# A hybrid decoder block with 32 experts: expert weights in 2 MiB transfers with 16 KiB per partition, a reordered model dimension, and a rearranged end

## The chip, the cores and the metric

The kernel runs on one core of one Trainium2 chip. The metric is the device time of one execution in microseconds; the time before is the median of three runs. Inputs and outputs are float32, and all weights are read from HBM once per execution.

## The reference

256 tokens (with 16 learned meta tokens ahead of them) go through a mixer, a mixture of experts and a last norm:

```
h    = concat(meta, x)                                  # 272 x 1024
proj = rmsnorm(h, norm_mix) @ w_in                      # u, q, k, v, two gates
ssm  = gated(gelu(s5_ssm(u)) , w_glu)                   # state-space branch
attn = sliding_window_attention(q, k, v, sinks)         # 16 heads, window 128
h    = h + (sig(g1) * (ssm @ w_br_ssm) + sig(g2) * (attn @ w_br_attn)) @ w_out
t    = rmsnorm(h, norm_ffn)
top 4 of 32 experts per token by t @ w_router + b_router, softmax over the four
for each expert e, for its tokens:
    g, up = split(t @ w_gate_up[e] + b_gate_up[e])      # 1024 x 2048 weights
    hid   = min(g, 7) * sigmoid(1.702 * min(g, 7)) * (clip(up, -7, 7) + 1)
    y     = hid @ w_down[e] + b_down[e]                 # 1024 x 1024 weights
h    = h + sum over the four experts of gate * y
out  = rmsnorm(h, norm_final)[16:]
```

An expert's weights are 8 MiB (w_gate_up) and 4 MiB (w_down), 384 MiB for all 32.

## The kernel before, in words

The program is written in the order in which each engine runs it; nothing reorders it.

**Mixer.** Five groups of matrix products (`Early` and `Block`, 34 + 40 steps) take their weights as units of 1 MiB. In the loop of L1090 over the steps n, a `Block` of the last product (kind `out`, w_out) adds its result to the residual stream `xt` in one VectorE instruction for each 256 columns (`e2`, L868); ScalarE squares follow (`e3`), then transposes of `xt` (`turn_out`, L889) and the router's logits.

**Expert phase.** The loop of L1397 runs `gate_up` for expert e and, inside and behind it, `hid_T`, `down` and `combine` of the experts before. Only the first 64 slots of an expert are computed in this loop, which is enough here. `gate_up` (L1265) takes 8 units of weights, 128 rows of w_gate_up each; for each unit TensorE runs two products for the gate half and two for the up half, and these two lie side by side in the array's columns. `down` (L1296) takes 4 units of two chunks (128 rows of w_down each) into one PSUM bank `py`; ScalarE copies its lower half and VectorE its upper half to `y`. After each second expert `combine` (L1317) multiplies both experts' `y` by the gates (four products of 128 rows) and VectorE adds them to `acc`. `group` gathers the tokens of two experts (L1246) between the units.

**The ring (L79).** All weights, the mixer's too, are a list `todo` of 1 MiB units, and a list of free slots (8 KiB on each of 128 partitions). `pump` gives the first free slot to the next unit and issues its DMA on SyncE's queue. `done` puts a slot back when the program has issued the last product on its unit, so that the DMA into it waits on TensorE. A row of w_gate_up is 8 KiB, so a unit of it is one run of 8 KiB per partition (`gu_unit`, L187); a unit of w_down has two runs of 4 KiB per partition (`dn_unit`, L190). Slots are handed to the ring where the mixer's buffers come free (L247, L249, L262, L766, L1089, L1136 to L1151, L1156); 18 of them serve the experts, and two more (`aA` at 0 and `late_`) only until they become `acc` and `y`. The DMA completions use eight semaphores in turn, so at most eight of SyncE's transfers are under way: an issue waits for the landing of the eighth before it, and the queue is in order, so whatever stands behind a waiting issue waits too. The last expert's last 1 MiB comes as two transfers of 512 KiB (`dn_half`).

**End (L1420, L1444).** Behind the last `gate_up` come the end of `down(30)`, `hid_T(31)`, the products that spread norm_final over the partitions (`nf_banks`), `down(31)`, `combine` of experts 30 and 31, squares, a root on GpSimd, and for each of two token tiles two VectorE products, one ScalarE and one VectorE scaling and two output DMAs on SyncE (`last`, L1374).

The program as it stands before the change, where the diff touches it:

Of the kernel before, what the change touches and what calls it, by code (L numbers as in the profile page):

```python
# [73 lines left out]
class Slot:  # L74
    def __init__(self, ap):
        self.ap, self.keep = ap, True


class Ring:  # L79


    def __init__(self, eng):
        self.eng = eng
        self.todo, self.held, self.free, self.used = [], [], [], 0

    def add(self, parts):
        self.todo.append(parts)
# [50 lines left out]
def hybrid_block(ctx: ExitStack, tc: tile.TileContext, x, meta, norm_mix, w_in, lam_re, lam_im, log_dt,  # L138
# [48 lines left out]
    def gu_unit(e, k):  # L187
        return [(lambda t: t, w_gate_up[0, e, 128 * k:128 * k + 128, :])]

    def dn_unit(e, q):  # L190
        ap = w_down[0, e, 256 * q:256 * q + 256, :].rearrange("(c p) n -> p c n", p=128)
        return [(lambda t: t.rearrange("p (c n) -> p c n", c=2), ap)]

    def dn_half(e, c):
        return [(lambda t: t[:, :D], w_down[0, e, 128 * c:128 * c + 128, :])]

    for e in range(n_exp + 1):
        if e < n_exp:
            for k in range(8):
                ring.add(gu_unit(e, k))  # L200
        if e:
            for q in range(3 if e == n_exp else 4):
                ring.add(dn_unit(e - 1, q))
    for c in (6, 7):
        ring.add(dn_half(n_exp - 1, c))
# [41 lines left out]
    r0_slots = ring.slots([r0(0, U_)])  # L247
    nc.sync.dma_start(out=ct[:, 128:], in_=consts[:, 128:])
    r0_slots += ring.slots([r0(U_, U_)])  # L249
# [12 lines left out]
    r0_slots += ring.slots([r0(U_ * 2, U_)])  # L262
# [57 lines left out]
    T.transpose(aux[:, 0:32], rows[:32], ident[:32, :32])  # L320
    vecs = cp.tile([128, 32], F32, name="vecs")
    V.tensor_copy(vecs, aux[:, 0:32])
    nmix, dsk, nffn, bglu = (vecs[:, 8 * i:8 * i + 8] for i in range(4))
# [27 lines left out]
    wbuf = [pK.tile([128, 2, 8 * 128], F32R, tag="pb", name=n, bufs=2) for n in ("wh", "wl")]  # L351
# [133 lines left out]
    G.dma_start(out=wr, in_=w_router[0].rearrange("(k p) e -> p k e", p=128))  # L485
# [207 lines left out]
    gt.append(pB.tile([128, 8, NT], F32, name="gt0"))  # L693
    Z, Sc, X = (Arena(pB, U_, n) for n in ("Z", "Sc", "X"))
# [71 lines left out]
    r0_slots += ring.slots([r0(4 * U_, U_)])  # L766
# [28 lines left out]
    def act_pair(name):  # L795
# [3 lines left out]
        else:  # L799
            act[name] = [pK.tile([128, 8, NT], F32R, tag="pb", name=name + p, bufs=2) for p in "hl"]  # L800

    class Block:
# [5 lines left out]
        def hi(self):  # L808
# [46 lines left out]
        def e2(self):  # L855
# [124 lines left out]
    gt.append(pD.tile([128, 8, NT], F32, name="gt1"))  # L980
    Q, Y0 = Arena(pD, U_, "Q"), Arena(pD, U_, "Y0")
    W2 = Arena(pD, U_, "W2")
# [106 lines left out]
    ring.slots([Q(0, U_), Y0(0, U_)])  # L1089
    for n in range(B + 2):  # L1090
# [46 lines left out]
        if n == N + 1:  # L1137
            s_y = ring.slots([late_])[0]
            ring.slots([a(0, U_) for a in (Sc, W2)])
            r0_slots += ring.slots([r0(3 * U_, U_)])  # L1140
        if n == 17:
            ring.slots([Z(0, U_)])
# [381 lines left out]
```

## Time and profile before

| | us |
|---|---|
| median of three runs (1275.23 to 1277.87) | 1277.65 |
| the profiled execution | 1276.19 |
| its span, first to last instruction | 1274.4 |
| TensorE busy (share of the span) | 1188.9 (93%) |
| VectorE, ScalarE, GpSimd busy | 447.5, 224.7, 55.3 |
| HBM read | 443.31 MB, 350 GB/s over the span |

A busy TensorE is not TensorE at its peak: matmuls are pipelined and the ends in the profile are modelled. Each column of the page's timeline is a fortieth of the span, 31.9 us. The experts' weights are 403 of the 443 MB read. The granted clock was 0.994 over the span, which is the upper of TensorE's two levels (2.4 GHz) nearly throughout.

### The profile page before, as it was taken

What the parts mean: (1) busy time and instruction counts of PE and PEld (TensorE: products, weight loads), DVE (VectorE), ACT (ScalarE), POOL (GpSimd) and SP (SyncE); (2) the same over time, 40 slices, a digit from 0 to 9 for tenths busy, and PEclk for the clock granted to TensorE, in tenths of its full rate; (3) what the DMA queues carried; (4) which work ended last, traced back from release to release, by engine and by line L of the source; (5) the groups of instructions that cost most, each with busy time, mean ns of one, the idle gap of its engine ahead of it and who ended that gap; (6) DMA issues with size and microseconds to landing.
All of it is one profiled execution on the core that took longest, in us unless ns stands there. A gap on an engine that the chain in (4) does not pass through costs nothing.

```text
span 1274.4 us, 17188 instructions
## 1 busy us (share of the span) xinstructions
PE 1188.9 (93%) x7132; PEld 582.1 (46%) x7133; DVE 447.5 (35%) x995; ACT 224.7 (18%) x469; POOL 55.3 (4%) x86
## 2 busy tenths in 40 slices
PE   8989999999899999999989898989898989999985
PEld 6968778899333333333323232323232323333321
DVE  5978467675312231222213131212121222212212
ACT  3354366643000000000000000000000000000001
POOL 3019000000000000000000000000000000000000
PEclk9999989999999999999999999999999999999998
DMA  9925364898799999999999999999999999999994
GB/s 186 242 68 165 102 191 143 168 378 319 287 389 416 414 416 416 415 416 416 417 416 417 415 417 417 417 416 417 417 416 416 416 417 416 416 416 416 416 416 167
DMA packets 129285, 447.28 MB, mean 351 GB/s; under 512 B 26401, under 2 KB 62481, under 8 KB 96434
## 3 DMA queue, kind: packets, MB, share of 16 engines
q1 hardware_dynamic: 128768, 445.67, 90.5%
q8 instruction: 58, 0.95, 0.3%
q0 software_dynamic: 432, 0.45, 0.2%
q14 instruction: 25, 0.20, 0.0%
q10 hardware_dynamic: 2, 0.00, 0.0%
HBM read 443.31 MB, written 2.79 MB: 350 GB/s over the span
## 4 chain that ended last, share of the span: by engine, by line
DMA 51%; PE 41%; DVE 5%; ACT 2%; issue 1%; SPq 0%; POOL 0%; DVEq 0%; ACTq 0%
DMA r<-in_w_gate_up_dram 11%; DMA ws<-in_w_down_dram 6%; PE pgt L1273 6%; DMA Sc<-in_w_gate_up_dram 6%; PE py L1308 6%; PE pup L1273 6%; DMA X<-in_w_down_dram 5%; DMA Y<-in_w_gate_up_dram 5%; DMA Z<-in_w_gate_up_dram 5%; PE pu L419 4%; DMA Q<-in_w_down_dram 3%; DMA ws<-in_w_gate_up_dram 3%; PE pu L843 2%; PE pg L1246 2%; PE pu L844 2%; PE pu L845 2%
## 5 line engine op out<-in xcount | busy, mean ns | idle before, releaser
L1281 DVE TENSOR_SCALAR gs<-pgt 128x512 f32<-128x512 f32 x32 | 22.0, 687 | 235.2 <-PE pgt L1273 235.2
L1247 DVE TENSOR_TENSOR xw<-pg,vecs 128x256 f32<-128x256 f32 x64 | 27.1, 424 | 204.2 <-PE pg L1246 204.2
L1313 DVE COPY late__1936<-py 64x512 f32<-64x512 f32 x32 | 22.2, 695 | 189.2 <-ACT late__1936 L1312 189.2
L1246 PEld LDWEIGHTS pg<-aA,xt 128*128 128x128 f32 x512 | 61.9, 191 | 53.5 <-issue 49.4
L1273 PE MATMUL pgt<-r,xw 128*64 128x512 f32 x292 | 77.5, 609 | 6.6 <-DMA r<-in_w_gate_up_dram 5.9
L1246 PE MATMUL pg<-aA,xt 128*128 128x128 f32 x512 | 73.8, 287 | 2.6 <-DVE aA L1236 2.2
L1273 PE MATMUL pup<-r,xw 128*64 128x512 f32 x292 | 75.0, 592 | 0.0
L1308 PE MATMUL py<-r,hT 128*64 128x512 f32 x272 | 63.1, 595 | 5.1 <-DMA r<-in_w_down_dram 5.1
L1321 PE MATMUL pc<-late__1936,gT 128*128 128x512 f32 x128 | 62.2, 618 | 1.4 <-DVE late__1936 L1313 1.4
L1323 DVE TENSOR_TENSOR aA<-aA,pc 128x512 f32<-128x512 f32 x60 | 41.2, 687 | 56.5 <-PE pc L1321 56.5
L1312 ACT ACTIVATE late__1936<-py 64x512 f32<-64x512 f32 x32 | 18.9, 590 | 239.1 <-PE py L1308 239.1
L1293 ACT ACTIVATE hT<-pt 128x512 f32<-128x512 f32 x32 | 19.1, 597 | 208.8 <-PE pt L1291 208.8
L1263 ACT ACTIVATE gT<-pt 128x512 f32<-128x512 f32 x16 | 9.6, 597 | 255.8 <-PE pt L1262 255.8
L1282 ACT ACTIVATE sgm<-gs 128x512 f32<-128x512 f32 x32 | 20.0, 626 | 168.2 <-DVE gs L1281 168.2
L1273 PE MATMUL pgt<-ws,xw 128*64 128x512 f32 x168 | 44.6, 609 | 5.2 <-DMA ws<-in_w_gate_up_dram 4.8
L1308 PE MATMUL py<-ws,hT 128*64 128x512 f32 x168 | 40.0, 597 | 4.1 <-DMA ws<-in_w_down_dram 4.0
L1273 PE MATMUL pup<-ws,xw 128*64 128x512 f32 x168 | 43.2, 592 | 0.0
L1378 POOL TENSOR_TENSOR rsf<-ssf,nhalf 128x1 f32<-128x1 f32 x2 | 1.1, 554 | 946.8 <-DVE ssf L1377 946.8
L1308 PE MATMUL py<-gt,hT 128*64 128x512 f32 x160 | 38.1, 597 | 4.0 <-DMA gt<-in_w_down_dram 4.0
L1321 PEld LDWEIGHTS pc<-late__1936,gT 128*128 128x128 f32 x128 | 20.4, 188 | 43.1 <-DVE aA L1323 21.0
L1273 PEld LDWEIGHTS pup<-r,xw 128*64 128x64 f32 x292 | 20.9, 137 | 41.8 <-issue 41.8
L1308 PEld LDWEIGHTS py<-r,hT 128*64 128x64 f32 x272 | 19.0, 136 | 39.6 <-issue 25.1
(407 smaller groups left out, 2084.2 us busy)
## 6 DMA issues: line engine op xcount, KB each, us to landing
r<-in_w_gate_up_dram SPq DMA_DIRECT2D x73, 1024.0 KB, 19.7
ws<-in_w_gate_up_dram SPq DMA_DIRECT2D x42, 1024.0 KB, 20.0
r<-in_w_down_dram SPq DMA_DIRECT2D x34, 1024.0 KB, 20.0
gt<-in_w_gate_up_dram SPq DMA_DIRECT2D x22, 1024.0 KB, 20.0
Z<-in_w_gate_up_dram SPq DMA_DIRECT2D x21, 1024.0 KB, 20.1
Y<-in_w_gate_up_dram SPq DMA_DIRECT2D x21, 1024.0 KB, 20.1
W<-in_w_gate_up_dram SPq DMA_DIRECT2D x21, 1024.0 KB, 19.2
ws<-in_w_down_dram SPq DMA_DIRECT2D x21, 1024.0 KB, 20.1
```

The costliest lines, as they stand in the source:

```text
L419: T.matmul(pu, x_[:, k], y_[:, k, c:], start=(p + k == 0), stop=(p == len(pairs) - 1 and k == 7))
L843: T.matmul(pu, self.a[:, k], hi[:, k], start=(k == 0), stop=False)
L844: T.matmul(pu, self.a[:, k], lo[:, k], start=False, stop=False)
L845: T.matmul(pu, self.b[:, k], hi[:, k], start=False, stop=(k == 7))
L1246: T.matmul(pg[:, j], xt[:, t, 128 * (k + j):128 * (k + j) + 128], oh[:, t], start=(t == 0), stop=(t == 1))
L1247: V.tensor_tensor(xe[:, k:k + 2], pg, nffn[:, k:k + 2, None].to_broadcast([128, 2, n]), op=OP.mult)
L1273: T.matmul(p_[64 * hf:64 * hf + 64], lhs, rhs[:, c + 512 * hf:c + 512 * hf + 512], start=False, stop=(k == 7), tile_position=(0, 64 * hf), ...
L1281: V.tensor_scalar(g, pg, LIMIT, None, op0=OP.min)
L1308: T.matmul(py[64 * pp:64 * pp + 64], lhs, rhs[:, 512 * hf:512 * hf + 512], start=(c == -1), stop=(c == 7), tile_position=(0, 64 * pp), ski ...
L1313: V.tensor_copy(y[64:, 1 - odd], py[64:])
L1321: T.matmul(pc, gT[:, hf, t], y[:, hf], start=True, stop=True)
L1323: V.tensor_tensor(acc[:, t, cs_], (acc if started else xt)[:, t, cs_], pc, op=OP.add)
```

## The change

Four things. **(1)** An expert's weights come as 2 MiB transfers where two slots that lie side by side are free together: w_gate_up as four units of 256 rows, w_down as two units of 512 rows. In a unit partition p takes rows 2p and 2p + 1 of w_gate_up (or 4p to 4p + 3 of w_down), which is one run of 16 KiB. Slots are joined into seven pairs; four slots stay single, and a unit that meets no free pair is loaded as two halves into two single slots, with 8 KiB per partition. **(2)** Because a partition now holds neighbouring rows, the model dimension and the hidden dimension are read in another order. For the model dimension, the columns of w_out are taken with a stride where they are split (`Block.hi`, `lo`), `e2` becomes two VectorE instructions into PSUM and a ScalarE copy into `xt`, norm_ffn is loaded and transposed once more at the start (`nf4`), and w_router is loaded in the same order. For the hidden dimension, the clamps of `gate_up` read PSUM with a stride, and `down` writes `y` back in natural order by a strided copy. **(3)** Some slots reach the ring later (the pair of `Sc` and `Z` at n = 17, those of `W2`, `gt` and `X` at n = 33). **(4)** The end: `hid_T(31)` runs inside `down(30)`, the products on norm_final inside `gate_up(31)`; expert 30's share of the last combine runs inside `down(31)`, behind its chunks 1 and 3, as two products of 64 rows in the two row halves of the array; `down(31)` uses two PSUM banks; expert 31's share follows; the last scaling is fused with the product by norm_final for one half, and one of the output DMAs goes to ScalarE's queue.

```diff
+    def join(self, ap, a, b):
+        a.mate, b.mate, a.pair, b.pair, a.first = b, a, ap, ap, True
...
     def pump(self):
-        while self.free and len(self.held) < len(self.todo):
-            sl = self.free.pop(0)
-            for dst, src in self.todo[len(self.held)]:
-                self.eng.dma_start(out=dst(sl.ap), in_=src)
-            self.held.append(sl)
+        while self.free and (self.half or self.todo):
+            alone = [sl for sl in self.free if sl.mate is None]
+            if self.half:
+                if not alone:
+                    return
+                self.load(alone[0], self.half)
+                self.half = None
+                continue
+            parts, halves = self.todo[0]
+            if halves is None:
+                split = [sl for sl in self.free if sl.mate not in self.free]
+                self.load((alone or split or self.free)[0], parts)
+            else:
+                both = [sl for sl in self.free if sl.first and sl.mate in self.free]
+                if both:
+                    sl = both[0]
+                    self.eng.dma_start(out=sl.pair, in_=parts)
...
+                elif alone:
+                    self.load(alone[0], halves[0])
+                    self.half = halves[1]
+                else:
+                    return
+            self.todo.pop(0)
...
-    def gu_unit(e, k):
-        return [(lambda t: t, w_gate_up[0, e, 128 * k:128 * k + 128, :])]
+    def gu_unit(e, q):
+        src = w_gate_up[0, e, 256 * q:256 * q + 256, :].rearrange("(p c) n -> p c n", c=2)
+        return (src.rearrange("p c n -> p (c n)"), [[(lambda t: t, src[:, c])] for c in range(2)])
...
+    nf4 = aA(8 * L + 512, 256)[:4]
+    nc.sync.dma_start(out=nf4, in_=norm_ffn.rearrange("l (k n) -> (l k) n", n=256))
...
-                V.scalar_tensor_tensor(xt[:, :, cs_], pus[self.i][:, :, :256], 0.5, xt[:, :, cs_], op0=OP.mult, op1=OP.add)
+                pu = pus[self.i][:, :, :256].rearrange("p t (c n) -> p t c n", c=2)
+                for c in range(2):
+                    V.scalar_tensor_tensor(pu[:, :, c], pu[:, :, c], 0.5,
+                                           xt[:, :, cs_].rearrange("p t (n c) -> p t c n", c=2)[:, :, c],
+                                           op0=OP.mult, op1=OP.add)
+                S.activation(xt[:, :, cs_], pus[self.i][:, :, :256], AF.Copy)
...
         if n == 24:
-            ring.slots([gt[0].rearrange("p a n -> p (a n)")])
+            for i in range(0, 4, 2):
+                ring.join(r0(U_ * i, 2 * U_), *(next(sl for sl in r0_slots if sl.n == i + j) for j in range(2)))
+            ring.pump()
...
         if n == 33:
-            ring.slots([gt[1].rearrange("p a n -> p (a n)"), X(0, U_)]
-                       + [pK.tile([128, U_], F32, tag="pb", name="ws", bufs=2) for _ in range(2)])
+            ring.pairs([a(0, 2 * U_) for a in (W2, b4[1])] + [pK.tile([128, 2 * U_], F32, tag="pb", name="ws2", bufs=1)])
...
-        V.tensor_scalar(g, pg, LIMIT, None, op0=OP.min)
+        V.tensor_scalar(gv, turned(pg), LIMIT, None, op0=OP.min)
...
-        S.activation(y[:64, odd], py[:64], AF.Copy)
-        V.tensor_copy(y[64:, 1 - odd], py[64:])
+            if mid:
+                mid(c)
+        S.activation(rows2(y[:64, odd]), cols2(py[0][:64]), AF.Copy)
+        V.tensor_copy(rows2(y[64:, 1 - odd]), cols2(py[1][64:]))
+
+    def combine_one(gT, y, b, then=None):
+        for t in range(2):
+            pcs = [bank("y", "pc"), bank("t", "pc")]
+            for hf in range(2):
+                r = slice(64, 128) if hf != b else slice(0, 64)
+                T.matmul(pcs[hf], gT[r, hf, t], y[r, hf], start=True, stop=True, tile_position=(r.start, 0))
...
+    def scale(t, nf):
+        o = spare[t][:, D:]
+        S.activation(cols2(o[:, :512]), rows2(spare[t][:, :512]), AF.Copy, scale=rsf[:, t:t + 1])
+        for q in range(2):
+            V.scalar_tensor_tensor(cols2(o[:, 512:])[:, q], rows2(acc[:, t, 512:])[:, q], rsf[:, t:t + 1],
+                                   rows2(nf[1])[:, q], op0=OP.mult, op1=OP.mult)
+        (S if t else nc.sync).dma_start(out=ov[:, t, :512], in_=o[:, :512])
+        nc.sync.dma_start(out=ov[:, t, 512:], in_=o[:, 512:])
```

Where the change moves instructions, first SyncE's queue from the first expert's weights to the first slot that this phase hands back. The names are the destination buffers. Before:

```order
L99 DMA Z<-in_w_gate_up_dram 128x2048
L99 DMA r_63<-in_w_gate_up_dram 128x2048 x2
L99 DMA aA<-in_w_gate_up_dram 128x2048 x2
L99 DMA Q<-in_w_gate_up_dram 128x2048
L99 DMA gt_1037<-in_w_gate_up_dram 128x2048
L99 DMA Y_1927<-in_w_gate_up_dram 128x2048
L99 DMA r_63<-in_w_gate_up_dram 128x2048
L99 DMA late__1936<-in_w_gate_up_dram 128x2048
L99 DMA Sc<-in_w_gate_up_dram 128x2048
```

And now:

```order
L115 DMA r_63<-in_w_gate_up_dram 128x2048 x2
L115 DMA aA<-in_w_gate_up_dram 128x2048 x2
L135 DMA QY<-in_w_gate_up_dram 128x4096
L115 DMA late__1935<-in_w_gate_up_dram 128x2048
L115 DMA r_63<-in_w_gate_up_dram 128x2048
L135 DMA r_63<-in_w_gate_up_dram 128x4096
L135 DMA Wgt<-in_w_gate_up_dram 128x4096
L135 DMA gtX<-in_w_gate_up_dram 128x4096
L135 DMA ws_3485<-in_w_gate_up_dram 128x4096
L135 DMA ZSc<-in_w_down_dram 128x4096
L115 DMA ws<-in_w_down_dram 128x2048
L115 DMA wx<-in_w_down_dram 128x2048
```

The first expert's weights come half as single MiB; its last MiB (the `r_63` behind `late_`) waits for the single ring slot, which the second w_out unit frees, and four pairs stand behind it. The 20 MiB up to `wx` are the same as before.

The same queue over one round of the ring in the steady part (18 MiB), now:

```order
L135 DMA ZSc<-in_w_down_dram 128x4096
L115 DMA ws<-in_w_down_dram 128x2048
L115 DMA wx<-in_w_down_dram 128x2048
L135 DMA r_63<-in_w_gate_up_dram 128x4096
L115 DMA aA<-in_w_gate_up_dram 128x2048
L115 DMA r_63<-in_w_gate_up_dram 128x2048
L135 DMA QY<-in_w_gate_up_dram 128x4096
L135 DMA r_63<-in_w_gate_up_dram 128x4096
L135 DMA Wgt<-in_w_down_dram 128x4096
L135 DMA gtX<-in_w_down_dram 128x4096
L135 DMA ws_3485<-in_w_gate_up_dram 128x4096
```

Seven of these eleven transfers are pairs of 2 MiB, four are single MiB; before there were 18 of 1 MiB.

Last, TensorE from the last expert's `down` on, now (`pc` L1405 is `combine_one`, `py` L1389 a chunk's products):

```order
L1389 MATMUL py<-r_63,hT 64x512 x4
L1405 MATMUL pc<-late__1935,gT 128x512 x2
L1389 MATMUL py<-r_63,hT 64x512 x4
L1405 MATMUL pc<-late__1935,gT 128x512 x2
L1389 MATMUL py<-aA,hT 64x512 x4
L1389 MATMUL py<-r_63,hT 64x512 x2
L1389 MATMUL py<-QY,hT 64x512 x2
L1405 MATMUL pc<-late__1935,gT 128x512 x4
```

Before, sixteen `py` products of `down(31)` stood together, with the products on norm_final and `hid_T(31)` ahead of them and four `pc` products of 128 rows behind.

## Rows read from the trace of the kernel before

**Rows 1.** The page, part 2: GB/s in 40 slices of the span.

```profile
GB/s 186 242 68 165 102 191 143 168 378 319 287 389 416 414 416 416 415 416 416 417 416 417 415 417 417 417 416 417 417 416 416 416 417 416 416 416 416 416 416 167
```

**Rows 2.** By stretch: length; PE, PEld, DVE, ACT, POOL busy; clock, DMA share, GB/s.

```profile
360.00:597.00 237.00, 234.34 (x1126) 87.94 (x1124) 59.93 (x127) 18.78 (x32) 0.00 (x0) 1.00 1.02 416
597.00:1240.00 643.00, 593.90 (x2710) 202.85 (x2708) 142.84 (x290) 43.12 (x74) 0.00 (x0) 1.00 1.02 416
...
1250.00:1257.00 7.00, 7.00 (x33) 2.29 (x33) 0.00 (x0) 0.00 (x0) 0.00 (x0) 1.00 0.45 182
```

**Rows 3.** The chain that ended last: start us, length us, what.

```profile
3.70 4.92 DMA aA<-in_b_glu_dram
...
471.75 7.21 PE py L1308 x34
...
525.55 7.21 PE py L1308 x34
...
597.46 20.13 DMA r<-in_w_gate_up_dram
...
1226.43 20.16 DMA wx<-in_w_down_dram
...
1251.07 7.23 PE py L1308 x34
```

**Rows 4.** DMA in 458:474 (w_gate_up alone), 448:454, 478:484, 508:514 (w_down alone).

```profile
DMA packets 918, 6.70 MB, mean 419 GB/s; under 512 B 100, under 2 KB 100, under 8 KB 100
...
DMA packets 628, 2.44 MB, mean 406 GB/s; under 512 B 33, under 2 KB 33, under 8 KB 628
...
DMA packets 629, 2.43 MB, mean 406 GB/s; under 512 B 35, under 2 KB 35, under 8 KB 629
...
DMA packets 635, 2.45 MB, mean 409 GB/s; under 512 B 36, under 2 KB 36, under 8 KB 635
```

**Rows 5.** DMA in 597:1240: all packets, then queues (packets, MB, share).

```profile
DMA packets 47817, 267.58 MB, mean 416 GB/s; under 512 B 4079, under 2 KB 4079, under 8 KB 26273
...
q1 hardware_dynamic: 47788, 267.19, 101.5%
q8 instruction: 21, 0.34, 0.2%
```

**Rows 6.** SyncE's queue as the expert phase begins: start us, length us, transfer.

```profile
296.65 0.33 SPq L99 DMA_DIRECT2D W<-in_w_gate_up_dram  x1
...
317.15 0.37 SPq L99 DMA_DIRECT2D wx<-in_w_down_dram  x1
325.69 0.34 SPq L99 DMA_DIRECT2D Z<-in_w_gate_up_dram  x1
...
342.24 0.33 SPq L99 DMA_DIRECT2D Y<-in_w_gate_up_dram  x1
...
363.60 0.34 SPq L99 DMA_DIRECT2D W<-in_w_gate_up_dram  x1
```

**Rows 7.** VectorE's timeline at the mixer's end.

```profile
314.93 0.69 DVE L868 SCALAR_TENSOR_TENSOR xt<-sc,xt 128x512 f32<-128x512 f32 x1 [2.18 <-PE sc L838]
```

**Rows 8.** The timeline of all engines at the end.

```profile
1249.09 1.98 PE L1367 MATMUL nf<-gt,ct 1*128 1x512 f32 x4
...
1257.25 1.02 PE L1308 MATMUL py<-Q,hT 128*64 128x512 f32 x4
...
1258.33 0.59 ACT L1312 ACTIVATE late__1936<-py 64x512 f32<-64x512 f32 x1 [8.47 <-PE py L1308]
...
1258.95 0.69 DVE L1313 COPY late__1936<-py 64x512 f32<-64x512 f32 x1 [9.01 <-ACT late__1936 L1312]
...
1259.70 3.89 PE L1321 MATMUL pc<-late__1936,gT 128*128 128x512 f32 x8 [1.42 <-DVE late__1936 L1313]
...
1260.86 0.69 DVE L1323 TENSOR_TENSOR aA<-aA,pc 128x512 f32<-128x512 f32 x1 [1.22 <-PE pc L1321]
...
1267.77 1.43 SPq L1384 DMA_DIRECT2D out_dram<-Sc  x2
```

More of the change, by code (lines that the diff above doesn't have):

```diff
@@ L75, in __init__ @@
     def __init__(self, ap):
-        self.ap, self.keep = ap, True
+        self.ap, self.keep, self.mate, self.pair, self.first = ap, True, None, None, False
 class Ring:
@@ L83, in __init__, with add_two @@
         self.eng = eng
-        self.todo, self.held, self.free, self.used = [], [], [], 0
+        self.todo, self.held, self.free, self.used, self.half = [], [], [], 0, None
     def add(self, parts):
-        self.todo.append(parts)
+        self.todo.append((parts, None))
+    def add_two(self, whole, halves):
+        self.todo.append((whole, halves))
     def slots(self, aps):
@@ L261, in hybrid_block @@
         raw.append(t)
-    r0_slots += ring.slots([r0(U_ * 2, U_)])
+    r0_slot(2)
     def rstd_of(ms, n):
@@ L765, in hybrid_block @@
         S.activation(k0[:, 4 * half:4 * half + 4], pk, AF.Copy)
-    r0_slots += ring.slots([r0(4 * U_, U_)])
+    r0_slot(4)
     snk8 = cp.tile([128, 20], F32, name="snk8")
@@ L1088, in hybrid_block @@
     sqp = pa.tile([128, 2, 4], F32, name="sqp")
-    ring.slots([Q(0, U_), Y0(0, U_)])
+    ring.pairs([d4[0](0, 2 * U_)])
     for n in range(B + 2):
@@ L1138, in hybrid_block @@
             s_y = ring.slots([late_])[0]
-            ring.slots([a(0, U_) for a in (Sc, W2)])
-            r0_slots += ring.slots([r0(3 * U_, U_)])
+            r0_slot(3)
         if n == 17:
-            ring.slots([Z(0, U_)])
+            ring.pairs([b4[0](0, 2 * U_)])
         if n == 22:
@@ L1399, in hybrid_block @@
         if e == n_exp - 1:
-            sl = next(sl for sl in ring.free if sl not in r0_slots)
-            ring.free.remove(sl)
-            nfr = sl.ap
-            S.dma_start(out=nfr[0:1, :D], in_=norm_final.rearrange("(o d) -> o d", o=1))
+            nfr = pm.tile([128, 512], F32, tag="gT", name="nfr", bufs=3)
+            for hf in range(2):
+                S.dma_start(out=nfr[32 * hf:32 * hf + 1], in_=norm_final[512 * hf:512 * hf + 512].rearrange("(o d) -> o d", o=1))
         if e < n_exp:
@@ L1429, in hybrid_block, with mid_d @@
                     V.memset(Y[f], 0.0)
-            down(HID.pop(f), ring_d(f == n_exp - 1), selrow(f), Y[f - f % 2], f % 2)
+            def mid_d(c):
+                if e == n_exp - 1 and c == 3:
+                    HID[e] = hid_T(HID[e])
+                if e == n_exp and c in (1, 3):
+                    next(one, None)
+            if e == n_exp:
+                one = combine_one(GT[f - 1], Y[f - 1], 0)
+            down(HID.pop(f), ring_d(f == n_exp - 1), selrow(f), Y[f - f % 2], f % 2, mid_d, f == n_exp - 1)
             for _ in pend if e % 2 else ():
@@ L1441, in hybrid_block, with sums @@
             more = nc.values_load(imax[0:1, 0:1], min_val=0, max_val=NT)
-    for e in sorted(GT):
-        combine(GT.pop(e), Y.pop(e), squares if not GT else None)
-    last(nf)
+    def sums(t):
+        if t == 0:
+            return
+        for tt in range(2):
+            for hf in range(2):
+                squares(tt, hf)
+        root(0)
+        for tt in range(2):
+            weigh(tt, nf)
+        root(1)
+        for tt in range(2):
+            scale(tt, nf)
+    assert list(GT) == [n_exp - 2]
+    for _ in combine_one(GT.pop(n_exp - 2), Y.pop(n_exp - 2), 1, sums):
+        pass
+    gT = pm.tile([128, 2, 2, 128], F32, tag="gT", name="gT", bufs=3)
     with tc.If(more > TS):
```

131 lines of the change are left out of this document (87 added, 44 removed).

## The prediction

> **What bounds the kernel now.** I read the page's timeline first: from the thirteenth slice on, the core's DMA moves 414 to 417 GB/s in every slice until the last [rows 1]. The table by stretch says the same with the engines beside it: from 360 to 1240 the DMA share is 1.02, while TensorE falls from 99% busy (360 to 597) to 92% (597 to 1240) [rows 2]. The chain of waits then says which of the two ends last. From 471.75 to 525.55 it runs on TensorE, and one pair of experts takes the 53.8 us between these two `down` pieces, 26.9 us an expert. At 597.46 it changes to DMA, and 32 pieces of some 20 us, each a 1 MiB transfer from issue to landing, lead to 1246.6 [rows 3]. So TensorE works off its backlog until 597, and from there the stream of weights sets the pace. But the DMA queue was full and never idle since 360: what counts is when the stream starts to be full, its bytes, its rate, and what follows its end. At 1251.07 the chain goes back to TensorE for `down(31)` and the end [rows 3].
>
> **The rate, by row length.** A count of packets in stretches that hold one kind of row gives the time of a packet on one of the 16 DMA engines. With w_down alone (4 KiB rows) three stretches of 6 us hold 1892 packets, of which 104 are the small ones of completions: 16 x 18 us / 1788 = 161.1 ns a row. With w_gate_up alone (8 KiB rows), 16 x 16 us / 818 = 313 ns [rows 4]. The long stretch checks this: 643 us x 16 less 0.2% for instruction loads, less 22194 rows of 4 KiB at 161.1 ns, over the 21515 rows of 8 KiB, is 311 ns [rows 5]. Two rows of 4 KiB thus take 9 to 11 ns more than one of 8 KiB. I read this as a fixed cost of a row and carry it on: a 16 KiB row takes 2 x 311 less 9 to 11, 611 to 613 ns. I take 613, which is 427.6 GB/s. Its ends: 611, and 622 if nothing is saved beyond 8 KiB.
>
> Per MiB and engine (64 KiB): w_gate_up took 8 x 311 = 2.488 us and w_down 16 x 161.1 = 2.578, in the mix of two to one 2.518. Now 14 of 18 MiB go as 4 x 613 = 2.452, and 4 as 2.488: 2.460. From 360 to about 1250 (the share is 1.02 up to 1240, and 0.45 behind 1250 [rows 2]), 890 / 2.518 = 353 MiB passed; 353 x 0.058 = **-20.5 us**. With 611 it is -22.6, with 622 it is -10.6.
>
> The rows show the mixed stream at 416 and single rows of 8 KiB at 419 GB/s [rows 2, 4], and no row shows more for long. The Trainium skill (HBM Reference, section Specifications (TRN2)) says that a core streaming alone measures about 425 GB/s, bounded by its 16 DMA engines. As a ceiling, that would make the gain an estimated 19 us instead of 20.5; by my sum the new mix runs just above it, at 426.
>
> **Whether the ring can keep the stream full.** In the steady part one round is 18 MiB as before, in eleven transfers. TensorE takes 26.9 us for an expert and the stream then 12 x 2.460 = 29.5, so TensorE still waits for data and hands slots back at once. A pair goes back when its second half is used, one unit (1.7 us) later than singles would, against more than 10 MiB, 25 us, still under way. I cost that at nothing; the cover is the up to eight transfers in flight, each now up to 2 MiB. TensorE's backlog lasts longer: before it shrank by 30.2 - 26.9 = 3.3 us an expert, now by 2.6, so TensorE's part of the chain reaches to about 660 instead of 597, far from the end.
>
> **The start of the stream, where the change costs.** Both versions load 20 MiB before the first slot comes back. Before, the last of them was issued at 317.15, and then the queue had nothing until 325.69 [rows 6]. Now the second MiB of one unit waits for a single slot until the second w_out unit is used (296.65, where `W` was), and 8 MiB in pairs stand behind it. That burst runs to about 319, the last 4 MiB to 328.7, which uses up the idle time; all are wanted later (the second expert from 342). In the next stretch 14 MiB are issued in both versions, before in 14 transfers from 325.69 to 363.60 [rows 6], each starting as it was issued; two retired slots make holes in both. Now the single slot used as the first expert's eighth unit comes back at 342.24 [rows 6] and the pair `QY`, free since 338.8, stands behind it; the last pair waits for its second half until 363.60 and brings 2 MiB where 1 MiB was left. Counted through transfer by transfer, the fourteenth MiB is in at 369.2 instead of 366.2: **+3.0 us**. From there TensorE frees a MiB per 1.7 us and the queue is full in both.
>
> Two delays move this whole start. At the mixer's end `e2` took 0.69 us [rows 7]; now two instructions of half the size (some 0.4 each) and a ScalarE copy (0.59 for 512 columns out of PSUM [rows 8], with a handover) stand before the last transposes; for the three earlier w_out units a step of 24 products covers it, for the last one nothing does: +0.8. At the beginning the chain starts at the loads of the norm rows [rows 3]; one more load (0.4 us of SyncE's queue) and two small transposes come ahead: +0.5, between 0 and 0.8. The start costs **+4.3 us**, between 2 and 5.
>
> **The end.** Of `last` and its neighbours: (a) `nf` (1.98 us) and `hid_T` no longer stand before `down(31)` [rows 8]. (b) But `down(31)` can start only when its first pair lands, and that is 2 MiB instead of 1. Behind it come 1 MiB and two halves, 2.49 + 2 x 1.29 = 5.07 us before the last landing T. From there TensorE needs 8 chunks of 0.86 us (7.23 us with the bias [rows 3]), and two pairs of 64-row products between them. Four products of 128 rows took 3.89 [rows 8], 0.97 each; a new pair costs 0.86 if its two row halves run side by side, as the two column halves of a chunk do, or 1.95 if not. I take the first, the nearer row. So the products end at T + 3.5 (or T + 5.7); before, with T about 1256.8 (the last products start at 1257.25), they ended at 1258.3, T + 1.5 [rows 8]. Loss 2.0, or 4.2. (c) VectorE's copy waited for ScalarE's [rows 8] and now does not: -0.6. Four adds, which took 3.5 us from 1260.86, each waiting for its product [rows 8], follow closely: -0.6. The fused scaling and the output DMAs on two queues (1.43 us for two on one [rows 8]): -0.8. Together **0.0 us**, between -1 and +2.2.
>
> The strided clamps and copies, the new norm_ffn order and the router's load cost nothing: an expert's clamps have all of the next `down`, 7.2 us, to be done, and VectorE is busy 22% of the time [rows 2].
>
> **The sum:** -20.5 + 4.3 + 0.0 = -16.2 us. Against the profiled execution, 1276.19, that is 1260.0. The median of the runs is 1.46 higher, so I expect **1261.5**. With the kind ends (611 ns, +2, -1) it is 1256.1, with the unkind ones (622, +5, +2.2) 1274.2. About 0.2%, 2.6 us, is what a measurement of this kernel can tell from no change.
>
> **Rivals.**
> *A. Nothing, or less than half, is saved beyond 8 KiB,* be it that the fixed cost of a row lies elsewhere or that a 2 MiB transfer is cut into 8 KiB packets after all, so that the change does not do what it says. Then only w_down gains: -10.6 + 4.3, a time near 1271.5; with 618.5 ns near 1267. The Trainium skill (DMA: Bandwidth & Descriptors, section Why small descriptors are slow (HBM only)) speaks for this: it puts the fixed overhead at some 3 cycles a packet and finds joining worth it only to 256 B; from its 850 MHz that is an estimated 3.5 ns, and 1267. The trace disagrees so far, with 9 to 11 ns between 4 and 8 KiB [rows 4, 5]. Chance 0.15.
> *B. A 16 KiB packet is slower than two of 8 KiB.* The one kind of 16 KiB packet in the trace, the instruction loads, takes 0.2% of 10288 us / 21, about 1 us [rows 5], though to another place and in turns with the weights. Each ns above 613 costs 353 x 4 x 14/18 = 1099 rows, 1.1 us; from 628 ns on the change is a loss, at 650 ns the time is 1302. Against it: 4 to 8 KiB shows no such bend. Chance 0.06.
> *C. TensorE becomes the bound,* if clamps or copies in the new order slow an expert by over 2.6 us, or a pair's late return starves the queue. A few us of the gain go; near 1270. Chance 0.04.
>
> **The numbers.** The forecast has 0.75, with its own range 1256 to 1267. Reaching to A's 1271 leaves out B, the unkind ends and a little below: 1255.5 to 1271.5. Faster by over 0.2%: 0.75, most of A and of C, less the unkind ends: 0.89; within 0.2%: 0.03; slower: 0.08.
>
> **What would show it.** In the profile after: half the stretch's 8 KiB packets gone, and the steady stretch at 425 to 428 GB/s instead of 416 (right), or 422 (A), or under 416 (B). The DMA share at 1.0 from about 365; under it later, C. The chain on DMA from about 660 to 1235, in pieces of 2 MiB. `down(31)` ending about 3.5 us behind the last landing, with pairs of `pc` in 0.9 us. A stream that fills by 363, or after 375, makes the start's term wrong.

## The result and the profile after

The changed kernel takes **1265.35 us** in the median of four runs (1264.22 to 1266.37), the kernel before 1277.63 beside it: a ratio of 0.9906, interval 0.9894 to 0.9918, or 12.3 us less. A second comparison (`c_after`, below) gave 1264.46 against 1277.69, 0.9891 (0.9875 to 0.9906), or 13.2 less. The forecast was 16.2 less and 1261.5, with a range from 1255.5 to 1271.5: the direction and the range hold, and 3 to 4 us of the expected gain are missing. The profiled execution took 1265.7 us with a span of 1263.9, 10.5 less than the one of before.

The page's line that answers to [rows 1], for the changed kernel:

```profile
GB/s 179 235 86 146 124 165 153 146 321 245 321 406 425 423 425 426 425 425 427 424 424 425 426 426 424 426 425 423 426 425 425 424 427 425 424 426 426 425 425 152
```

The table by stretch, with the columns of [rows 2]:

```profile
320.00:337.00 17.00, 15.65 (x77) 8.43 (x76) 7.41 (x34) 0.67 (x4) 0.96 (x2) 0.80 0.90 355
337.00:360.00 23.00, 21.12 (x108) 8.43 (x110) 5.00 (x13) 3.11 (x4) 0.00 (x0) 1.00 0.79 301
360.00:597.00 237.00, 234.34 (x1128) 88.23 (x1126) 60.40 (x128) 18.18 (x31) 0.00 (x0) 1.00 1.01 425
597.00:1220.00 623.00, 578.44 (x2684) 209.76 (x2682) 142.19 (x289) 43.01 (x73) 0.00 (x0) 0.99 1.01 425
```

And the packets of the long stretch, as in [rows 5]:

```profile
DMA packets 22222, 264.84 MB, mean 425 GB/s; under 512 B 2470, under 2 KB 2470, under 8 KB 2472
...
q1 hardware_dynamic: 22192, 264.45, 100.5%
```

The steady stream runs at 425 GB/s instead of 416, in half the packets. Of the 19750 large ones some 12580 are of 16 KiB and 7170 of 8 KiB, by their sum of bytes. 623 us x 16 less 0.2%, less 7170 x 311.5 ns, leaves 613 ns for one of 16 KiB, by the same working as the forecast's and with the same result.

Two things in the first of these fences are new: the granted clock of 0.80 from 320 to 337, where before it was at its upper level, and a DMA share of only 0.79 from 337 to 360. The same two stretches before:

```profile
320.00:337.00 17.00, 14.78 (x83) 7.26 (x84) 5.93 (x23) 1.88 (x2) 0.00 (x0) 1.00 0.60 230
337.00:360.00 23.00, 21.55 (x112) 8.68 (x110) 4.93 (x11) 1.23 (x2) 0.00 (x0) 1.00 0.94 335
```

SyncE's queue there, which answers to [rows 6] (start, length, transfer):

```profile
298.76 0.33 SPq L115 DMA_DIRECT2D r<-in_w_gate_up_dram  x1
...
320.04 0.33 SPq L115 DMA_DIRECT2D wx<-in_w_down_dram  x1
333.28 0.33 SPq L135 DMA_DIRECT2D r<-in_w_gate_up_dram  x1
340.01 0.33 SPq L115 DMA_DIRECT2D aA<-in_w_gate_up_dram  x1
346.87 0.33 SPq L115 DMA_DIRECT2D r<-in_w_gate_up_dram  x1
347.25 0.43 SPq L135 DMA_DIRECT2D QY<-in_w_gate_up_dram  x1
...
368.24 0.33 SPq L135 DMA_DIRECT2D ws<-in_w_gate_up_dram  x1
```

The queue stands 2.1 us later than before at 298, 2.9 at `wx`, and 4.6 for the slots that came back at 342.24 and 363.60. The first refill is 7.6 later, since it is now a pair and waits for two slots. The half that waits (346.87), with the pair `QY` behind it, is where the forecast put it. The mixer's end, on VectorE and then on TensorE, says where the delay grows:

```profile
316.91 0.90 DVE L936 SCALAR_TENSOR_TENSOR sc<-sc,xt 128x256 f32<-128x256 f32 x2 [2.25 <-PE sc L904]
```

```profile
318.56 0.66 PE L960 MATMUL pt<-ct,xt 128*128 128x128 f32 x4 [0.94 <-ACT xt L939]
...
324.63 3.78 PE L1317 MATMUL pg<-aA,xt 128*128 128x128 f32 x16 [0.42 <-DVE aA L1307]
```

TensorE waits 0.94 us for the new ScalarE copy. Six microseconds later the first gather's sixteen products take 3.78 us instead of 2.05: they run at the lower of the two levels of the clock (1.2 GHz), which is granted from 321.5 to 328.3. The prediction had nothing there.

The chain, from where it passes to the DMA queue, and its end:

```profile
541.28 30.10 DMA r<-in_w_gate_up_dram
571.45 35.81 DMA ZSc<-in_w_down_dram
...
735.33 1.08 PE pgt L1344 x4
...
1027.41 5.38 PE py L1389 x16
...
1206.15 5.02 PE py L1389 x16
...
1215.99 24.52 DMA r<-in_w_down_dram
1240.65 1.94 PE py L1389 x8
1242.59 1.06 PE pc L1405 x4
```

On the way it goes back to TensorE three times (735 to 740, 1027 to 1047, 1206 to 1216), where the next issue waits for a slot that TensorE has yet to free. The stream loses nothing by it: its share stays at 1.01.

And the end on the timeline, answering to [rows 8]:

```profile
1249.13 1.03 PE L1389 MATMUL py<-QY,hT 128*64 128x512 f32 x4
1250.19 0.59 ACT L1395 ACTIVATE late__1935<-py 64x512 f32<-64x512 f32 x1 [10.43 <-PE py L1389]
1250.23 0.69 DVE L1396 COPY late__1935<-py 64x512 f32<-64x512 f32 x1 [2.34 <-PE py L1389]
1250.98 1.99 PE L1405 MATMUL pc<-late__1935,gT 64*128 64x512 f32 x8 [0.82 <-DVE late__1935 L1396]
1252.14 2.48 DVE L1408 TENSOR_TENSOR aA<-aA,pc 128x512 f32<-128x512 f32 x4 [1.21 <-PE pc L1405]
...
1257.65 0.33 SPq L1487 DMA_DIRECT2D out_dram<-Wgt  x1
```

`down(31)` starts when its first 2 MiB land and ends at 1250.2. The weights' last packet ended at 1245.1, so that is T + 5.1. From there 13.8 us pass to the end of the span; before they were 16.2.

### The profile page after: what moved, and what is told of

Same layout as the page of the kernel before. It is cut to its first block, busy times and chain, and to the rows that moved or that the text cites. A ratio compares the mean times of both kernels' runs of the same rounds, so it can differ in the third digit from the quotient of the medians.

```text
span 1263.9 us, 16923 instructions
## 1 busy us (share of the span) xinstructions
PE 1183.1 (94%) x7142; PEld 593.7 (47%) x7143; DVE 450.5 (36%) x1004; ACT 227.4 (18%) x473; POOL 55.2 (4%) x86
## 4 chain that ended last, share of the span: by engine, by line
DMA 53%; PE 39%; DVE 5%; ACT 2%; issue 1%; SPq 0%; POOL 0%; DVEq 0%; ACTq 0%
DMA r<-in_w_gate_up_dram 10%; DMA ws<-in_w_gate_up_dram 5%; DMA ws<-in_w_down_dram 5%; PE py L1389 5%; PE pgt L1344 5%; DMA gtX<-in_w_down_dram 5%; DMA aA<-in_w_down_dram 5%; PE pup L1344 5%; DMA QY<-in_w_down_dram 5%; DMA r<-in_w_down_dram 4%; PE pu L481 4%; DMA wx<-in_w_gate_up_dram 3%; DMA ZSc<-in_w_down_dram 3%; DMA wx<-in_w_down_dram 3%; DMA Wgt<-in_w_gate_up_dram 2%; DMA Wgt<-in_w_down_dram 2%
## 5 line engine op out<-in xcount | busy, mean ns | idle before, releaser
L1344 PE MATMUL pgt<-r,xw 128*64 128x512 f32 x380 | 102.0, 615 | 18.3 <-DMA r<-in_w_gate_up_dram 18.3
L1344 PE MATMUL pup<-r,xw 128*64 128x512 f32 x380 | 99.4, 602 | 0.0
L1344 PE MATMUL pgt<-ws,xw 128*64 128x512 f32 x208 | 54.8, 605 | 6.0 <-DMA ws<-in_w_gate_up_dram 6.0
L1344 PEld LDWEIGHTS pup<-r,xw 128*64 128x64 f32 x380 | 27.5, 139 | 55.7 <-issue 55.7
L1344 PE MATMUL pup<-ws,xw 128*64 128x512 f32 x208 | 53.5, 592 | 0.0
L1389 PE MATMUL py<-QY,hT 128*64 128x512 f32 x164 | 40.3, 636 | 8.7 <-DMA QY<-in_w_down_dram 8.7
L1344 PEld LDWEIGHTS pgt<-r,xw 128*64 128x64 f32 x380 | 22.4, 136 | 50.4 <-DMA r<-in_w_gate_up_dram 27.1
L1389 PE MATMUL py<-ZSc,hT 128*64 128x512 f32 x176 | 39.8, 593 | 3.4 <-DMA ZSc<-in_w_down_dram 3.4
L1389 PE MATMUL py<-gtX,hT 128*64 128x512 f32 x160 | 36.2, 594 | 3.5 <-DMA gtX<-in_w_down_dram 3.5
L1389 PE MATMUL py<-Wgt,hT 128*64 128x512 f32 x160 | 36.2, 593 | 3.4 <-DMA Wgt<-in_w_down_dram 3.4
```

Source lines behind the costliest of these rows:

```text
L1344: T.matmul(p_[64 * hf:64 * hf + 64], lhs, rhs[:, c + 512 * hf:c + 512 * hf + 512], start=False, stop=(k == 7), tile_position=(0, 64 * hf), ...
L1389: T.matmul(py[pp][64 * pp:64 * pp + 64], lhs, rhs[:, 512 * hf:512 * hf + 512], start=(c == -1), stop=(c == 7), tile_position=(0, 64 * pp), ...
```

## Experiments

Readings that recur below, all from the profiled execution of each run, in us: A, the start of the mixer's last product (`sc`); B, from there to the last four transposes; C, from those to the first expert's first product, with the first gather in between (in brackets: its sixteen products on the timeline); D, from that product to the moment when 300 MiB were still to be moved (counted back from the last packet, packets of 4 KiB and more); E, from the last packet of weights to the end of the last `py` product. `e8_split`, whose stream ran at half the rate, is left out.

| run | A | B | C (gather) | D | E | span |
|---|---|---|---|---|---|---|
| before | 314.6 | 1.06 | 8.05 (2.05) | 173.3 | 1.97 | 1274.4 |
| `c_before` | 316.5 | 1.07 | 8.06 (2.05) | 173.7 | 3.62 | 1277.8 |
| after | 316.5 | 2.04 | 9.79 (3.78) | 173.4 | 5.06 | 1263.9 |
| `c_after` | 316.5 | 2.04 | 9.78 (3.78) | 172.9 | 5.03 | 1263.9 |
| `e1_clock` | 314.8 | 2.03 | 9.78 (3.78) | 173.2 | 5.03 | 1261.8 |
| `e2_one` | 320.6 | 1.12 | 9.67 (3.67) | 173.0 | 5.04 | 1266.7 |
| `e3_eager` | 314.0 | 2.03 | 9.72 (3.72) | 172.9 | 5.06 | 1260.9 |
| `e4_last` | 316.3 | 2.04 | 9.74 (3.74) | 173.3 | 3.62 | 1261.9 |
| `e5_one_late` | 314.4 | 1.07 | 8.04 (2.05) | 173.2 | 5.05 | 1258.7 |
| `e6_eager_late` | 314.3 | 2.04 | 9.71 (3.71) | 171.4 | 5.06 | 1259.5 |
| `e7_rows8` | 314.3 | 2.03 | 9.64 (3.62) | 174.9 | 5.05 | 1272.4 |
| `e9_gap` | 313.8 | 1.73 | 9.13 (3.12) | 173.7 | 5.06 | 1260.7 |
| `e10_all` | 314.8 | 1.07 | 8.05 (2.05) | 171.5 | 3.77 | 1255.7 |

D is nearly the same in before and after, because by then the faster stream has won back what the pairs lost. A has two levels, 313.8 to 314.8 and 316.1 to 316.5, which no edit explains: the kernel before shows both. So spans are compared here by B to E and not by A, and the times by their ratio to the kernel before, run beside each. The intervals of `e4_last`, `e5_one_late`, `e6_eager_late` and `e9_gap` overlap that of `c_after`, so what these four runs show rests on B to E.

**The two kernels again** (`c_after`, `c_before`), no edit.

> The changed kernel once more, as a base for the runs beside it. Both theories expect the result again, 1264 to 1266.5 us. What is asked is whether the clock falls again behind the mixer's last products. Theory (the longer gap that e2 makes there lets the granted clock fall): the sixteen products of the first gather take about 3.8 us again, instead of 2.05 in the kernel before, and the first expert's first products start at 328 to 329. Rival (the fall was a chance of that one execution): the sixteen products take about 2.05, the first expert starts near 326.5 and the time is 1.7 us lower.

> The kernel before once more, for a second profile. Theory (the changed program, not chance, makes the clock fall behind the mixer): the gather's sixteen products take 2.05 us again, with a granted clock of 1.00 from 320 to 337. Rival (chance): about 3.7 us, as in the changed kernel. It also shows by how much the first 300 us differ between two executions of one program.

Measured: `c_after` as above, with the gather at 3.78 us and a clock of 0.80 again. `c_before` in one run 1279.56 us; its products:

```profile
317.53 0.66 PE L889 MATMUL pt<-ct,xt 128*128 128x128 f32 x4
...
323.61 2.05 PE L1246 MATMUL pg<-aA,xt 128*128 128x128 f32 x16 [0.76 <-DVE aA L1236]
...
1253.07 3.38 PE L1308 MATMUL py<-Z,hT 128*64 128x512 f32 x8
```

So the fall behind the mixer belongs to the changed program. But of the 4.6 us by which its expert phase starts later than in [rows 6], 1.9 are two executions of one program apart. Its own `down(31)` shows a fall of the clock too (3.38 us for products that took 1.89 in the first profile), so E is 3.62.

**Idle products in the gap** (`e1_clock`):

```
+        if n == B:
+            keep_clock(tr_bank(), b3[:, :128], b3[:, :416], 4)
         if at(-1):
             at(-1).turn_out()
```

> Four idle products (0.7 us of TensorE) are put into the gap that TensorE has between the mixer's last products and the last transposes; nothing else. Theory (the gap lets the clock fall, and the fall costs 1.7 us in the gather): the gather's sixteen products go back from 3.8 to about 2.05 us, the granted clock of the stretch 320 to 337 from 0.80 to 1.00, the first expert starts 1.7 us earlier, and since each us of this start is a us at the end, the time falls by 1.7 us. Rival (the gather is slow for another reason, or the start does not carry through to the end): no change within 0.5 us, or the idle products only delay the transposes by up to 0.3 us.

Measured: 1264.2 us, 0.9894 (0.9879 to 0.9909), no difference from `c_after`.

```profile
315.73 0.87 PE L344 MATMUL pt<-b 96*128 96x416 bf16 x4
316.84 0.66 PE L960 MATMUL pt<-ct,xt 128*128 128x128 f32 x4 [0.23 <-ACT xt L939]
...
322.91 3.78 PE L1319 MATMUL pg<-aA,xt 128*128 128x128 f32 x16 [0.41 <-DVE aA L1309]
```

The gap is filled to 0.23 us and the clock falls all the same. A miss: either the gap is not the cause, or idle products don't stand for real ones there.

**One VectorE instruction for the last unit** (`e2_one`): the residual's last 256 columns are put into the new order ahead, through a PSUM bank, as the last unit's products begin.

```
                     pus[self.i] = bank2()
+                    if self.i == 3:
+                        S.activation(pus[3][:, :, 256:].rearrange("p t (c n) -> p t c n", c=2),
+                                     xt[:, :, 768:].rearrange("p t (n c) -> p t c n", c=2), AF.Copy)
+                        S.activation(xt[:, :, 768:], pus[3][:, :, 256:], AF.Copy)
...
+                if self.i == 3:
+                    V.scalar_tensor_tensor(xt[:, :, cs_], pus[3][:, :, :256], 0.5, xt[:, :, cs_], op0=OP.mult, op1=OP.add)
+                    return
```

> For the last w_out unit the residual is put into the new column order ahead of time by two ScalarE copies, so that e2 is one VectorE instruction again, without the copy behind it. Theory (e2's two instructions and the copy cost 0.9 us on the path, and the gap they make costs 1.7 us more through the clock): the last transposes start 0.9 us earlier, the gather takes about 2.05 us, and the time falls by 2.6 us. Rival 1 (e2 costs its 0.9 us, the clock has nothing to do with it): -0.9 us and a gather of 3.8 us. Rival 2 (ScalarE's two copies come in the way of the mixer's last steps): no gain.

Measured: 1269.13 us, 0.993 (0.9917 to 0.9944), slower than `c_after`. Rival 2: the copies use the bank that the next products write, and stand in ScalarE's queue behind the work of the unit before.

```profile
312.94 0.38 PE L906 MATMUL sc<-wh,mh 128*128 128x256 f32 x1 [2.94 <-ACT xt L899]
...
327.76 3.67 PE L1324 MATMUL pg<-aA,xt 128*128 128x128 f32 x16 [0.75 <-DVE aA L1314]
```

TensorE waits 2.94 us in the middle of the products. B is back at 1.12, but the gather still runs at the lower level. The granted clock fell behind that wait, was back at its upper level by 318, and fell again at 327.8, although from the last transposes to the gather every product and every wait is as in the kernel before. So a gap ahead of these transposes is not needed for the fall; whether the first fall brought the second was not tried.

**The same, six steps earlier** (`e5_one_late`): the two copies at n = 34 through a bank of the transposes (`tr_bank`).

> As the run on e2 before, but the two ScalarE copies that turn the residual's last columns go through another PSUM bank and six steps earlier, so that no product waits for them. Theory (the gap of 0.9 us that e2 makes lets the clock fall): no gap ahead of the last transposes, the gather's sixteen products in 2.05 us, 2.7 us less from the mixer's last product to the first expert's first. Rival (the clock falls there for another reason): 0.9 us less, the gather still takes 3.7 us.

Measured: 1262.9 us, 0.9875 (0.9859 to 0.9892).

```profile
315.48 0.66 PE L963 MATMUL pt<-ct,xt 128*128 128x128 f32 x4
...
321.54 2.05 PE L1324 MATMUL pg<-aA,xt 128*128 128x128 f32 x16 [0.75 <-DVE aA L1314]
```

B and C are those of the kernel before, 2.7 us less in all, as expected: 1.0 for `e2` and 1.7 for the clock.

**The gap put back by itself** (`e9_gap`), on top of `e5_one_late`:

```
                     V.scalar_tensor_tensor(xt[:, :, cs_], pus[3][:, :, :256], 0.5, xt[:, :, cs_], op0=OP.mult, op1=OP.add)
+                    S.activation(xt[:, :, cs_], xt[:, :, cs_], AF.Copy)
                     return
```

> As the run with the residual turned six steps earlier, and with one more ScalarE instruction behind e2 that copies the last 256 columns onto themselves and that the last transposes wait for: a gap of about 0.75 us, where that run has none. Theory (the gap ahead of the last transposes lets the clock fall, at 1.7 us): the transposes 0.75 us later, the gather's sixteen products 3.7 us instead of 2.05, and 2.4 us in all from the last product to the first expert's first. Rival (two VectorE instructions, or something else in the changed e2, does it): 0.75 us and a gather of 2.05 us.

Measured: 1264.67 us, 0.9895 (0.988 to 0.991).

```profile
315.55 0.66 PE L964 MATMUL pt<-ct,xt 128*128 128x128 f32 x4 [0.63 <-ACT xt L936]
...
321.62 3.12 PE L1325 MATMUL pg<-aA,xt 128*128 128x128 f32 x16 [0.76 <-DVE aA L1315]
324.68 1.61 PE L1352 MATMUL pgt<-r,xw 128*64 128x512 f32 x4
```

A gap of 0.63 us, where the run without the copy has none, brings the fall back. It sets in later, inside the gather, and lasts into the first expert's first products (1.61 us for what took 1.08). B and C grow by 0.66 and 1.09 together, 1.75 us where 2.4 were expected, and the first expert's first products by 0.53: 2.3 us in all. In the fourteen profiles the gather takes 3.1 to 3.8 us in the eight with a wait of 0.6 us or more ahead of the last transposes, and 2.05 in four of the six without. So such a gap is enough, whatever makes it. It is not the whole cause: with the gap filled by idle products (`e1_clock`) and without one (`e2_one`) the clock falls too, and why stays open.

**Halves at the start** (`e3_eager`): up to the second expert's end a slot whose mate is not free counts as single.

```
-            alone = [sl for sl in self.free if sl.mate is None]
+            alone = [sl for sl in self.free if sl.mate is None or self.eager and sl.mate not in self.free]
...
     for e in range(n_exp + 1):
+        ring.eager = e < 2
```

> Up to the second expert's end a unit that meets no free pair is loaded as two halves into slots whose mate is not free, too, as soon as each is free; later pairs as before. Theory (of the late start 3 us come from pairs that go back whole and from the half that waits with others behind it): the first refill is issued 2 to 3 us earlier, the DMA share of the stretch 337 to 360 rises from 0.79 to above 0.9, the steady rate stays at 425 GB/s, and the time falls by 2.5 to 3 us. Rival (the start is set by TensorE's pace in the first expert alone, so that earlier issues only wait): within 0.5 us. What speaks against a full gain: some 20 MiB more come in rows of 8 KiB, 0.2 us.

Measured: 1263.33 us, 0.9889 (0.9874 to 0.9904): no difference that can be told. The share from 337 to 360 did rise to 0.91, but where the ring goes back to pairs SyncE's queue shows

```profile
379.01 0.33 SPq L115 DMA_DIRECT2D aA<-in_w_down_dram  x1
388.33 0.33 SPq L115 DMA_DIRECT2D r<-in_w_down_dram  x1
```

a half that waits 9.3 us for the other single slot, with everything behind it. Already in the mixer the singles had lost their places next to each other. What was won was lost again (D 172.9).

**Halves only from the first expert on** (`e6_eager_late`): the same with `eager` off until the expert loop begins.

> Halves into slots whose mate is not free only from the first expert's first product on, not in the mixer, so that the single slots keep their places in the ring. Theory (the first such run won 1.7 us by the second expert and lost it when it went back to pairs, since a half had to wait 9 us for a single slot that had lost its place): the gain of about 2 us over the base stays, as the distance from the first expert's first product to the point where 300 MiB are left: 171 us instead of 173.1 in the base. Rival (going back to pairs always costs what was won, because one half waits): 172.9 or more.

Measured: 1261.61 us, 0.987 (0.9853 to 0.9886); D 171.4 instead of 172.9 to 173.4, and the gather at 3.71. So 1.5 to 2 us of the start come from slots that go back as pairs and from the half that waits.

**The last pair as two transfers** (`e4_last`):

```
-            ring.add_two(*dn_unit(e - 1, 0))
...
+    for h in dn_unit(n_exp - 1, 0)[1]:
+        ring.add(h)
```

> The last expert's first unit of w_down comes as two transfers of 1 MiB into two slots instead of one of 2 MiB; nothing else. Theory (the last down starts when its first transfer lands, and a 2 MiB one lands one MiB, 2.46 us, later than it could be used): the last down starts within 0.3 us of the end of the one before, about 1.3 us earlier against the last landing, and the time falls by 1.3 us (2.4 at most, if nothing else held it). Rival (TensorE is held by the last landing or by the work between the chunks, whatever its start): within 0.5 us.

Measured: 1263.77 us, 0.9877 (0.9861 to 0.9894).

```profile
1238.47 0.39 PE L1390 MATMUL py<-b,sel 96*64 96x512 bf16 x2
1238.69 1.89 PE L1390 MATMUL py<-r,hT 128*64 128x512 f32 x8
```

`down(31)` follows its bias without a wait. E falls from 5.05 to 3.62, 1.4 us, as expected; the times' intervals alone would not show it.

**8 KiB runs in 2 MiB transfers** (`e7_rows8`):

```
-        return (src.rearrange("p c n -> p (c n)"), [[(lambda t: t, src[:, c])] for c in range(2)])
+        return (w_gate_up[0, e, 256 * q:256 * q + 256, :].rearrange("(c p) n -> p c n", c=2), [[(lambda t: t, src[:, c])] for c in range(2)])
...
-                    self.eng.dma_start(out=sl.pair, in_=parts)
+                    self.eng.dma_start(out=sl.pair.rearrange("p (a n) -> p a n", a=2), in_=parts)
```

> The pairs stay transfers of 2 MiB, but each is two runs of 8 KiB per partition (rows p and p + 128, or two neighbouring rows of w_down in each half of the unit), so that the weights meet the wrong rows of the activations: the products are as many and as large as before, their sums are other ones. Theory (the gain in rate is a fixed cost of a row, so it goes with the length of the run): from 360 on all packets are 8 KiB at 311 to 312 ns, the stream falls from 425 to about 420 GB/s (2.466 to 2.494 us a MiB), and the time rises by 353 x 0.028 = 10 us. Rival (the gain comes with transfers of 2 MiB, fewer issues and landings): 425 GB/s and no change.

Measured: 1275.87 us, 0.9982 (0.9973 to 0.9991), 11.4 above `c_after`. Its stretches:

```profile
360.00:597.00 237.00, 234.33 (x1126) 88.27 (x1127) 60.42 (x128) 18.18 (x31) 0.00 (x0) 1.00 1.01 420
597.00:1220.00 623.00, 567.75 (x2646) 205.67 (x2646) 139.50 (x285) 43.00 (x73) 0.00 (x0) 0.99 1.01 420
```

And the packets of the long stretch, none of them of 16 KiB but the 21 instruction loads:

```profile
DMA packets 34347, 261.56 MB, mean 420 GB/s; under 512 B 2441, under 2 KB 2441, under 8 KB 2441
```

Between 340 and 5 MiB left a MiB takes 2.498 us, against 2.466 after and 2.519 before. 353 x 0.032 = 11.2 us: the whole difference. The trace's own duration of an 8 KiB packet has a median of 313 ns here, mostly in transfers of 2 MiB, as it has before and after in transfers of 1 MiB; one of 16 KiB has 614 after the change. The gain belongs to the run's length, not to the transfer's size.

**16 KiB runs in 1 MiB transfers** (`e8_split`):

```
-                    self.eng.dma_start(out=sl.pair, in_=parts)
+                    for r in (slice(0, 64), slice(64, 128)):
+                        self.eng.dma_start(out=sl.pair[r], in_=parts[r])
```

> Each pair is issued as two transfers of 1 MiB, of 64 partitions each, with 16 KiB per partition as before; nothing else. Theory (length of the run): 16 KiB packets at 613 to 614 ns and 425 GB/s; the time within 1 us of the base. Rival (size of the transfer): the stream falls back towards 418 GB/s, and the time rises by 10 us or more. What could disturb: eight transfers under way are now at most 8 MiB.

Measured: 2109.75 us, a ratio of 1.6522 (1.6435 to 1.6608). Neither theory had this.

```profile
597.00:1220.00 623.00, 386.27 (x1376) 131.58 (x1376) 71.23 (x147) 21.85 (x37) 0.00 (x0) 0.81 1.01 223
```

All DMA engines are busy (1.01) and move 223 GB/s: each packet takes about twice as long (a median of some 1190 ns for 16 KiB, and 605 for the 8 KiB ones, which still go to 128 partitions). The run changed the partitions with the size, so it says nothing on size; `e7_rows8` does.

**All three** (`e10_all`): the edits of `e5_one_late`, `e6_eager_late` and `e4_last` together.

> Three edits together: the residual turned early, halves at the expert phase's start, the last w_down pair as two transfers. Theory (their effects lie one behind the other on the one path): -2.7 - 1.75 - 1.45 = -5.9 us against the base, near 1258.5 us, a ratio of 0.985 to the kernel before. Rival (an earlier start of TensorE meets a queue that is not ready, so that the first two cover each other): -3.5 to -4.5 us.

Measured: **1257.87 us** (1257.44 to 1259.51), 0.9843 (0.983 to 0.9857), which is faster than both kernels: its interval touches neither of the changed kernel's.

```profile
320.00:337.00 17.00, 14.59 (x81) 7.15 (x82) 6.12 (x24) 1.88 (x2) 0.00 (x0) 1.00 0.97 393
337.00:360.00 23.00, 21.54 (x112) 8.79 (x110) 4.94 (x11) 1.23 (x2) 0.00 (x0) 1.00 0.95 360
360.00:597.00 237.00, 234.34 (x1118) 87.88 (x1116) 59.99 (x127) 18.18 (x31) 0.00 (x0) 0.99 1.01 425
```

Against `c_after` B and C are 2.7 shorter, D 1.4 to 1.9, E 1.3, and the ratios are 6.1 us apart: the effects add.

## Why the prediction was right, and where it was off

| term | forecast | measured |
|---|---|---|
| rate | -20.5 | -18.8 (2.519 to 2.466 us a MiB, x 353) |
| start: pairs and the half that waits | +3.0 | +2.1 to 2.9 |
| start: `e2` | +0.8 | +1.0 |
| start: fall of the clock behind `e2` | not seen | +1.7 |
| start: load and transposes at the beginning | +0.5 | within the two levels of A |
| end | 0.0 | +0.7 or -0.8 |
| sum | -16.2 | -12.5 (before and after), -14.8 (`c_before` and `c_after`) |

The spans themselves, each less its A, are 12.4 and 13.9 us apart; 0.9 of the second pair is not accounted for.

**The rate** was read rightly, with its cause: the packet of 16 KiB at 613 ns, rival A's fixed cost elsewhere (422 GB/s) and B (packets over 628 ns) out. Two rows of 8 KiB (some 312 ns each by `e7_rows8`) take about 11 ns more than one of 16 KiB, much as two of 4 KiB against one of 8. By the Trainium skill (DMA: Bandwidth & Descriptors, section Why small descriptors are slow (HBM only)) it would be an estimated 3.5; the measurement decides. Of the 18.8 us, 11.2 belong to the step to 16 KiB, the rest to w_down's step to 8. The forecast's 2.460 us a MiB became 2.466: this term was 1.7 us too large. The Trainium skill's 425 GB/s (HBM Reference, section Specifications (TRN2)) is what the steady stretch shows, and the 426 of my sum is not reached.

**The start** failed in one step: the sum priced the wait behind `e2` (+0.8, measured 1.0) at its length alone. The wait also lets TensorE's clock fall, 1.7 us more (`e5_one_late` takes it away, `e9_gap` brings most of it back). Together with the 1.7 of the rate this is most of what the forecast missed. The pairs' +3.0 was about right, if a little large: from the first expert's first product to 340 MiB left before took 72.7 and 72.9, after 74.8 and 74.3 although 14 MiB by then came 0.7 faster, and `e6_eager_late`, without whole pairs there, has 72.6. The load at the beginning can't be told apart: A is 316.5 in `c_before` and in after.

**The end** was forecast at 0.0 and came out at +0.7 against the first profile of before; that it is so near is luck, since its parts were further off. `down(31)` ended at T + 5.1, not T + 3.5: its first pair let it start 4.45 us ahead of T instead of 5.07, two pairs of `pc` take 1.06 of TensorE's time each instead of 0.86, and the eight chunks, broken up by them, 7.44 instead of 6.88. Before, T was 1256.3 and not 1256.8, so that `down(31)` ended at T + 2.0 there: the loss is 3.1 instead of 2.0. What follows was shortened by 2.4 instead of 2.0. In `c_before`, where the clock fell in `down(31)`, E is 3.62, and against it the end is worth -0.8.

**The chain** passed to the DMA queue at 541, not near 660, and went back to TensorE for short stretches. My step counted TensorE's backlog in MiB only. That TensorE starts 4.6 us later and that a pair lands as a whole, 2.46 us later for its first half, may both have used it up sooner; what each did was not measured. It cost nothing, since the queue was full anyway. Rival C did not happen.

## What to carry to other kernels

Where one queue streams weights without a pause, count its bytes by length of run: each row cost a fixed 10 ns or so here, and 16 KiB instead of 8 in seven ninths of the bytes was worth 1.3% of the stream, at one size of transfer. Price a wait that is added to TensorE at its length and once more by what the clock does behind it: look at the granted clock of the stretch behind the wait, too. Larger units cost time at both ends of a stream, so keep small ones there (`e10_all`) and large ones in between.

## What the hardware did that I had not expected

A wait of 0.6 to 0.9 us ahead of four transposes was followed by a fall of the clock some 3 to 7 us behind it, for about 1.7 us of extra time, and four idle products in that wait did not prevent it. In one run (`e2_one`) the clock fell at the same place without that wait.

With every pair cut into two transfers of 64 partitions the stream moved 223 GB/s instead of 425, with every DMA engine busy, and the transfers of 128 partitions in between slowed down too. The Trainium skill has this (SBUF — State Buffer, section Door 1: The DMA port swizzle (why `[64,N]` ≈ `[32,N]`)): partitions 0 to 63 reach only half of the ports, with an asymptote of about 218 GB/s. The trace agrees, at 223; I had not drawn on it when I wrote the expectation.

Two executions of one program differ by 1.9 us at the mixer's end (314.6 and 316.5), and the thirteen profiles in which nothing ahead of that point was disturbed lie near one or the other. Between before and `c_before` TensorE is 0.7 us apart by 28 us, 1.5 by 157 and 1.8 by 172. What decides was not tried.
